# Seven-product stage: the upper weight part meets both parts of the rows in one 512-column matmul

## Chip, cores and metric

The kernel runs on one core of a Trainium2 chip. The metric is the device time of one execution in microseconds, here the median of three runs.

## What is computed

One layer of an encoder over 512 rows of 2048 channels, in float32: an RMS norm, one input projection into eight parts, a short gated convolution (branch A), a diagonal complex state-space recurrence (branch B), a gated merge, an output projection with a residual, and a final RMS norm. The change lies in branch A, which needs four of the projections (v, bg, cg, za), each 2048 x 2048:

```python
h = rmsnorm(x, norm_g)
proj = jnp.einsum('bld,dn->bln', h, w_in)
v, bg, cg, za, u, zb, ga, gb = jnp.split(proj, SPLITS, axis=-1)
ya = bg * causal_depthwise_conv(cg * v, conv_w)
ya = jnp.einsum('blc,cd->bld', ya * jax.nn.silu(za), w_out_a)
...
m = jax.nn.sigmoid(ga) * ya + jax.nn.sigmoid(gb) * yb
return x + jnp.einsum('bld,de->ble', m, w_o)
```

## The kernel before

Channels lie on the 128 partitions, the 512 rows (`L`) on the free axis. Every float32 product is made of three: a weight is split into an upper part `w_hi` (rounded, cast on ScalarE, line 544) and a lower part `w_lo` (the rest, subtracted on VectorE, line 561), and the rows into an upper and a lower part that lie side by side in one tile (`pair`, 128 x 2 x 512; `h_comb`, 128 x 2 x 2 x 256). Upper by upper, upper weight by lower rows, and lower weight by upper rows are summed in PSUM; the fourth is dropped. A weight tile `w_raw` of 128 x 1024 holds eight slices of 128 x 128; `WStream` loads it, casts and subtracts some products ahead, with four buffers each for `w_hi` and `w_lo`, so that the cast for the fourth product after this one waits until this one's last use of its `w_hi`.

The four projections of branch A take a stage of their own, after the gating products of branch B and the products of `wgb` (whose background work builds the combined rows) and before the products of `wga`. For a pair of column tiles (256 channels) a projection is a 2 x 2 block product: two halves of the 2048 inner channels, two halves of the 512 rows. Instead of eight block products it takes seven, with sums of weights (lines 491 to 500, on VectorE) and sums of rows (`T1` to `T4`, made in `combine` as `h_sum`, `h_t`, `h_comb`). `product` (line 911) multiplies one weight tile by 256 rows, eight slices of three matmuls of 256 columns. `seven` (line 921) calls it seven times: `pb`, `pd` and `pa` are halves of PSUM banks that several products share, running on without being cleared, and after each product ScalarE copies or VectorE adds its bank into a quarter of the result `o`. Eight pairs of column tiles times four projections make 32 calls of `seven`.

Behind each product one piece of background work is issued (`step`): the convolution (`conv`), the gate (`silu`), the gating and the write to DRAM (`out_a`). At the stage's end the eight results `yag` are read back from DRAM and split (`reload`, tiles `yag_r`), while four gate products run.

The engines work through their own instruction lists in order; a scheduler writes these lists and assigns buffers from pools. Of the pools, `tp` has five tiles of 128 x 512 (`tmp`), `r4b` four of 128 x 1024 (`wide`), opened when `uyp` closes after branch B; `psp` has the eight PSUM banks.

Of the kernel before, what the change touches and what calls it, by code (L numbers as in the profile page):

```python
# [16 lines left out]
P = 128  # L17
L = 512
# [559 lines left out]
def hybrid_kernel(ctx: ExitStack, tc: tile.TileContext, xT, x, cvec, fg, wu, wu7, wabc,  # L578
# [8 lines left out]
    tp = ctx.enter_context(tc.tile_pool(name="tp", bufs=5))  # L587
# [3 lines left out]
    uyp = tc.tile_pool(name="uyp", bufs=1)  # L591
    uyp_ctx = uyp.__enter__()

    def psum():
        t = psp.tile([P, L], F32, tag="ps", name="ps")
        return t

    c.psum = psum

    def tmp():  # L600
        t = tp.tile([P, L], F32, tag="tmp", name="tmp")
        return t
# [234 lines left out]
    for m in range(8):  # L837
        ps = psum()
        gemm(ps, yg)
        th, g = tmp(), tmp()  # L840
        act.activation(th, ps, AF.Tanh, scale=0.25, bias=bgh[:, m:m + 1])
        tt(g, yg[m][:, 0].bitcast(F32), yg[m][:, 1].bitcast(F32), ADD)
        stt(g, th, 1.0, g, ADD, MUL)
        tt(g, g, zb[m], MUL)
        b = pair()
        split(b, g)
        yb.append(b)
    uyp.__exit__(None, None, None)
    r4b = ctx.enter_context(tc.tile_pool(name="r4b", bufs=4))

    def wide(name, shape=(P, 2, L)):
        t = r4b.tile(list(shape), F32, tag="r4", name=name)
        return t
# [57 lines left out]
    def product(ps, acts, first, last):  # L911
        hi, lo = W.get()
        hi, lo = (w.rearrange("p (k n) -> p k n", n=P) for w in (hi, lo))
        for k in range(8):
            a = acts[k]
            nc.tensor.matmul(ps, hi[:, k], a[:, 0], start=first and k == 0, stop=False, skip_group_check=True)  # L916
            nc.tensor.matmul(ps, hi[:, k], a[:, 1], start=False, stop=False, skip_group_check=True)  # L917
            nc.tensor.matmul(ps, lo[:, k], a[:, 0], start=False, stop=last and k == 7, skip_group_check=True)  # L918
        step()

    def seven(name):

        o = wide(name)
        o11, o12, o21, o22 = o[:, 0, :HL], o[:, 0, HL:], o[:, 1, :HL], o[:, 1, HL:]
        pb, pd, pa = (psum()[:, :HL] for _ in range(3))
        product(pb, Y11, True, False)
        act.copy(o11, pb)
        product(pd, T1, True, False)
        act.copy(o22, pd)
        product(pb, T2, False, False)  # L930
        act.copy(o12, pb)
        product(pd, Y22, False, True)
        tt(o12, pd, o12, ADD)
        product(pb, T3, False, False)
        tt(o22, pb, o22, ADD)
        product(pa, Y21, True, True)
        tt(o11, pa, o11, ADD)
        product(pb, T4, False, True)
        act.copy(o21, pb)
# [247 lines left out]
```

## Time and profile before

| | |
|---|---|
| median of three runs | 1718.92 us (1717.94 to 1720.54) |
| the profiled execution | 1717.99 us |
| its span, first to last instruction | 1716.2 us |
| seven-product stage in it | 691.8 to 1337.2 us |
| busy, share of the span: TensorE, VectorE, ScalarE | 99%, 67%, 38% |

The profile shows one execution. A matmul row's duration reaches from its start to the end of its last column's way through the array, so neighbouring rows overlap, and the pace is read from start to start. VectorE's rows overlap a little in the same way. PEld is the loading of a weight slice into the array. "Idle before" names what ended the idle time of an engine. Names: `ps` is a PSUM bank, `w_sum` a tile with a sum of weights, `tmp`, `zb`, `cg`, `v`, `za`, `bg` SBUF tiles.

### The profile page before, as it was taken

The page shows a single profiled execution, that of the slowest core. Times are in us where ns is not written, and L with a number is a line of the kernel's source. Part 1 is how long each engine was busy: PE and PEld are TensorE (multiplying, and loading weights), DVE is VectorE, ACT ScalarE, POOL GpSimd, SP SyncE. Part 2 cuts the span into 40 slices and gives each one's busy share as a digit, 9 for nine tenths or more (in the row PEclk, how much of TensorE's full clock was granted, in tenths as well). Part 3 has the DMA queues.
Part 4 walks back from the last instruction along what each step waited for, and adds up shares of the span by engine and source line. Part 5 has one row for each costly group of instructions (what it writes and reads, how often), then busy time and mean ns, then how long its engine had stood idle before and what let it go on. Part 6 is the DMA issues. An engine that isn't in the chain of part 4 may idle for free.

```text
span 1716.2 us, 25344 instructions
## 1 busy us (share of the span) xinstructions
PE 1703.9 (99%) x10308; PEld 1530.4 (89%) x10308; DVE 1142.6 (67%) x1717; ACT 657.5 (38%) x883; POOL 130.5 (8%) x224
## 2 busy tenths in 40 slices
PE   9999999999999999999999999999999999999998
PEld 7888888888888888999999999999999888888887
DVE  7894584849759855687877777777878533333333
ACT  6434433233335422344444444444444422223321
POOL 0004212130100111000000000000000100010000
PEclk9999999999999999999999999999999999999999
DMA  8324334444441553333333333333344943363212
GB/s 299 123 86 130 126 121 114 146 123 142 124 122 50 184 160 129 105 99 119 114 119 121 108 111 99 111 111 123 102 129 132 340 158 111 111 234 124 78 43 98
DMA packets 65269, 222.18 MB, mean 129 GB/s; under 512 B 8896, under 2 KB 9024, under 8 KB 65152
## 3 DMA queue, kind: packets, MB, share of 16 engines
q1 hardware_dynamic: 49392, 170.94, 30.5%
q0 software_dynamic: 15040, 48.53, 9.1%
q8 instruction: 80, 1.31, 0.3%
q10 hardware_dynamic: 720, 1.10, 0.2%
q14 instruction: 37, 0.30, 0.1%
HBM read 195.24 MB, written 21.10 MB: 126 GB/s over the span
## 4 chain that ended last, share of the span: by engine, by line
PE 98%; DMA 1%; DVE 1%; ACT 0%; issue 0%; DVEq 0%; SPq 0%; ACTq 0%
PE ps L690 15%; PE ps L691 15%; PE ps L692 15%; PE ps L916 12%; PE ps L917 12%; PE ps L918 12%; PE ps L1040 3%; PE ps L1042 3%; PE ps L1041 3%; PE ps L767 1%; PE ps L768 1%; PE ps L769 1%; PE ps L338 1%; PE ps L433 1%; PE ps L347 1%; DMA yag_r<-yag 0%
## 5 line engine op out<-in xcount | busy, mean ns | idle before, releaser
L561 DVE TENSOR_TENSOR w_lo<-w_raw,w_hi 128x1024 fp32r<-128x1024 f32 (+2 forms) x341 | 412.6, 1213 | 340.8 <-ACT w_hi L544 340.5
L544 ACT CAST w_hi<-w_raw 128x1024 fp32r<-128x1024 f32 (+2 forms) x341 | 355.1, 1042 | 732.7 <-PE ps L691 368.4
L690 PE MATMUL ps<-pair,w_hi 128*128 128x512 f32 x1104 | 430.4, 390 | 0.0
L692 PE MATMUL ps<-pair,w_lo 128*128 128x512 f32 x1104 | 429.1, 389 | 0.6 <-DVE w_lo L561 0.6
L691 PE MATMUL ps<-pair,w_hi 128*128 128x512 f32 x1104 | 429.4, 389 | 0.0
L916 PE MATMUL ps<-h_comb,w_hi 128*128 128x256 f32 x1024 | 289.9, 283 | 0.1
L918 PE MATMUL ps<-h_comb,w_lo 128*128 128x256 f32 x1024 | 289.8, 283 | 0.0
L917 PE MATMUL ps<-h_comb,w_hi 128*128 128x256 f32 x1024 | 289.8, 283 | 0.0
L692 PEld LDWEIGHTS ps<-pair,w_lo 128*128 128x128 f32 x1104 | 207.2, 188 | 44.2 <-DVE w_lo L561 1.1
L690 PEld LDWEIGHTS ps<-pair,w_hi 128*128 128x128 f32 x1104 | 207.3, 188 | 42.7
L691 PEld LDWEIGHTS ps<-pair,w_hi 128*128 128x128 f32 x1104 | 207.3, 188 | 42.2
L917 PE MATMUL ps<-pair,w_hi 128*128 128x256 f32 x768 | 217.3, 283 | 0.0
L918 PE MATMUL ps<-pair,w_lo 128*128 128x256 f32 x768 | 217.3, 283 | 0.0
L916 PE MATMUL ps<-pair,w_hi 128*128 128x256 f32 x768 | 217.3, 283 | 0.0
L916 PEld LDWEIGHTS ps<-h_comb,w_hi 128*128 128x128 f32 x1024 | 196.6, 192 | 0.3 <-DVE bg L47 0.3
L917 PEld LDWEIGHTS ps<-h_comb,w_hi 128*128 128x128 f32 x1024 | 196.6, 192 | 0.0
L918 PEld LDWEIGHTS ps<-h_comb,w_lo 128*128 128x128 f32 x1024 | 196.6, 192 | 0.0
L916 PEld LDWEIGHTS ps<-pair,w_hi 128*128 128x128 f32 x768 | 147.5, 192 | 0.0
L917 PEld LDWEIGHTS ps<-pair,w_hi 128*128 128x128 f32 x768 | 147.5, 192 | 0.0
L918 PEld LDWEIGHTS ps<-pair,w_lo 128*128 128x128 f32 x768 | 147.5, 192 | 0.0
L544 ACT CAST w_hi<-w_sum 128x1024 fp32r<-128x1024 f32 x64 | 67.2, 1049 | 123.7 <-PE ps L917 114.9
L561 DVE TENSOR_TENSOR w_lo<-w_sum,w_hi 128x1024 fp32r<-128x1024 f32 x64 | 78.2, 1223 | 44.1 <-ACT w_hi L544 44.1
(204 smaller groups left out, 1909.2 us busy)
## 6 DMA issues: line engine op xcount, KB each, us to landing
w_raw<-in_wabc_dram SPq DMA_DIRECT2D x128, 512.0 KB, 3.6
w_raw<-in_wga_dram SPq DMA_DIRECT2D x64, 512.0 KB, 3.9
w_raw<-in_wgb_dram SPq DMA_DIRECT2D x48, 512.0 KB, 4.1
w_raw<-in_wo_dram SPq DMA_DIRECT2D x32, 512.0 KB, 3.6
w_raw<-in_wgz_dram SPq DMA_DIRECT2D x24, 512.0 KB, 3.7
w_raw<-in_wu_dram SPq DMA_DIRECT2D x15, 448.0 KB, 7.9
xt<-in_xT_dram SPq DMA_DIRECT2D x16, 256.0 KB, 6.8
ga<-tmp POOLq DMA_DIRECT2D x16, 256.0 KB, 2.3
```

The source lines that it names most:

```text
L338: nc.tensor.matmul(ps[:, i * NCH:(i + 1) * NCH], self.sl[ri][:, q].rearrange("p g s -> p (g s)"), self.u4[:, q, :], start=True, stop=True)
L544: nc.scalar.copy(hi[:, a:b], raw[:, a:b])
L561: nc.vector.tensor_tensor(out=lo[:, a:b], in0=raw[:, a:b], in1=hi.bitcast(F32)[:, a:b], op=SUB)
L690: nc.tensor.matmul(ps, hi[:, k], a[:, 0], start=first and k == 0, stop=False)
L691: nc.tensor.matmul(ps, hi[:, k], a[:, 1], start=False, stop=False)
L692: nc.tensor.matmul(ps, lo[:, k], a[:, 0], start=False, stop=last and k == 7)
L916: nc.tensor.matmul(ps, hi[:, k], a[:, 0], start=first and k == 0, stop=False, skip_group_check=True)
L917: nc.tensor.matmul(ps, hi[:, k], a[:, 1], start=False, stop=False, skip_group_check=True)
L918: nc.tensor.matmul(ps, lo[:, k], a[:, 0], start=False, stop=last and k == 7, skip_group_check=True)
L1040: nc.tensor.matmul(ps, a[:, 0, cs], hi[:, k2, c0:c1], start=first and k2 == 0, stop=False)
L1041: nc.tensor.matmul(ps, a[:, 0, cs], lo[:, k2, c0:c1], start=False, stop=False)
L1042: nc.tensor.matmul(ps, a[:, 1, cs], hi[:, k2, c0:c1], start=False, stop=last and k2 == 1)
```

## The change

`product` now multiplies a slice of the upper weight by both parts of the rows in one matmul of 512 columns: the upper rows go to the first half of a bank, the lower rows to the second. The lower weight's matmul adds 256 columns onto the second half. A product therefore fills a whole bank, and its value is the sum of the two halves. `seven` copies and adds whole banks into two scratch tiles (`half`: `e1`, `e2`) and adds the halves only at the end, with one operation for each column tile, into `o`. For the scratch tiles the pool `r4b` has six tiles instead of four; the pool `tp` is closed before it opens, and `tmp` then takes tiles of `r4b`.

```diff
-    tp = ctx.enter_context(tc.tile_pool(name="tp", bufs=5))
...
+    uyp, tp = tc.tile_pool(name="uyp", bufs=1), tc.tile_pool(name="tp", bufs=5)
+    uyp_ctx, tp_ctx = uyp.__enter__(), tp.__enter__()
+    r4b = None
...
     def tmp():
-        t = tp.tile([P, L], F32, tag="tmp", name="tmp")
+        if r4b:
+            return wide("tmp")[:, 0]
+        t = tp_ctx.tile([P, L], F32, tag="tmp", name="tmp")
         return t
...
+    tp.__exit__(None, None, None)
     uyp.__exit__(None, None, None)
-    r4b = ctx.enter_context(tc.tile_pool(name="r4b", bufs=4))
...
+    r4b = ctx.enter_context(tc.tile_pool(name="r4b", bufs=6))
...
     def product(ps, acts, first, last):
         hi, lo = W.get()
         hi, lo = (w.rearrange("p (k n) -> p k n", n=P) for w in (hi, lo))
+        both = ps.rearrange("p (h l) -> p h l", h=2)
         for k in range(8):
             a = acts[k]
-            nc.tensor.matmul(ps, hi[:, k], a[:, 0], start=first and k == 0, stop=False, skip_group_check=True)
-            nc.tensor.matmul(ps, hi[:, k], a[:, 1], start=False, stop=False, skip_group_check=True)
-            nc.tensor.matmul(ps, lo[:, k], a[:, 0], start=False, stop=last and k == 7, skip_group_check=True)
+            nc.tensor.matmul(both, hi[:, k], a, start=first and k == 0, stop=False,
+                             skip_group_check=True)
+            nc.tensor.matmul(both[:, 1], lo[:, k], a[:, 0], start=False, stop=last and k == 7,
+                             skip_group_check=True)
         step()
...
-        o11, o12, o21, o22 = o[:, 0, :HL], o[:, 0, HL:], o[:, 1, :HL], o[:, 1, HL:]
-        pb, pd, pa = (psum()[:, :HL] for _ in range(3))
+        e1, pb = wide("half"), psum()
         product(pb, Y11, True, False)
-        act.copy(o11, pb)
+        act.copy(e1[:, 0], pb)
+        e2, pd = wide("half"), psum()
         product(pd, T1, True, False)
-        act.copy(o22, pd)
+        act.copy(e2[:, 1], pd)
         product(pb, T2, False, False)
-        act.copy(o12, pb)
+        act.copy(e1[:, 1], pb)
         product(pd, Y22, False, True)
-        tt(o12, pd, o12, ADD)
+        tt(e1[:, 1], pd, e1[:, 1], ADD)
         product(pb, T3, False, False)
-        tt(o22, pb, o22, ADD)
+        tt(e2[:, 1], pb, e2[:, 1], ADD)
+        pa = psum()
         product(pa, Y21, True, True)
-        tt(o11, pa, o11, ADD)
-        product(pb, T4, False, True)
-        act.copy(o21, pb)
+        tt(e1[:, 0], pa, e1[:, 0], ADD)
+        for i, e in enumerate((e1, e2)):
+            if i:
+                product(pb, T4, False, True)
+                act.copy(e2[:, 0], pb)
+            v = e.rearrange("p b (h l) -> p b h l", h=2)
+            tt(o[:, i].rearrange("p (b l) -> p b l", b=2), v[:, :, 0], v[:, :, 1], ADD)
         return o
```

TensorE's list where one product ends and the next begins, before (the rows of a product are `pair` or `h_comb`):

```order
L916 MATMUL ps<-pair,w_hi 128x256
L917 MATMUL ps<-pair,w_hi 128x256
L918 MATMUL ps<-pair,w_lo 128x256
L916 MATMUL ps<-h_comb,w_hi 128x256
L917 MATMUL ps<-h_comb,w_hi 128x256
L918 MATMUL ps<-h_comb,w_lo 128x256
```

and now:

```order
L924 MATMUL ps<-pair,w_lo 128x256
L922 MATMUL ps<-pair,w_hi 128x512
L924 MATMUL ps<-pair,w_lo 128x256
L922 MATMUL ps<-h_comb,w_hi 128x512
L924 MATMUL ps<-h_comb,w_lo 128x256
```

Three matmuls for each slice have become two, a long and a short one in turn.

VectorE's list in one call of `seven`, from the sum of weights behind the third product, before:

```order
L491 TENSOR_TENSOR w_sum<-w_raw 128x1024
L47 TENSOR_TENSOR cg<-ps,cg 128x256
L495 TENSOR_TENSOR w_raw<-w_raw 128x1024
L561 TENSOR_TENSOR w_lo<-w_raw,w_hi 128x1024
L47 TENSOR_TENSOR cg<-ps,cg 128x256
L496 TENSOR_TENSOR w_raw<-w_sum,w_raw 128x1024
L561 TENSOR_TENSOR w_lo<-w_sum,w_hi 128x1024
L47 TENSOR_TENSOR cg<-ps,cg 128x256
L500 TENSOR_TENSOR w_sum<-w_raw 128x1024
L561 TENSOR_TENSOR w_lo<-w_raw,w_hi 128x1024
L561 TENSOR_TENSOR w_lo<-w_sum,w_hi 128x1024
```

and now:

```order
L47 TENSOR_TENSOR half<-ps,half 128x512
L561 TENSOR_TENSOR w_lo<-w_raw,w_hi 128x1024
L495 TENSOR_TENSOR w_raw<-w_raw 128x1024
L47 TENSOR_TENSOR half<-ps,half 128x512
L496 TENSOR_TENSOR w_raw<-w_sum,w_raw 128x1024
L561 TENSOR_TENSOR w_lo<-w_sum,w_hi 128x1024
L47 TENSOR_TENSOR half<-ps,half 128x512
L500 TENSOR_TENSOR w_sum<-w_raw 128x1024
L47 TENSOR_TENSOR cg<-half 128x512
L561 TENSOR_TENSOR w_lo<-w_raw,w_hi 128x1024
L47 TENSOR_TENSOR cg<-half 128x512
L561 TENSOR_TENSOR w_lo<-w_sum,w_hi 128x1024
```

The three additions out of PSUM are twice as wide, and two additions of halves (`cg<-half`) stand before and behind a subtraction for lower weights.

VectorE's list at the end of the stage, in the last `seven` (result `bg`), before:

```order
L47 TENSOR_TENSOR pair<-yag_r,pair 128x512 x2
L47 TENSOR_TENSOR bg<-ps,bg 128x256
L47 TENSOR_TENSOR pair<-yag_r,pair 128x512
L561 TENSOR_TENSOR w_lo<-w_raw,w_hi 128x1024
L47 TENSOR_TENSOR pair<-yag_r,pair 128x512
```

and now:

```order
L47 TENSOR_TENSOR bg<-half 128x512
L561 TENSOR_TENSOR w_lo<-w_raw,w_hi 128x1024 x2
L47 TENSOR_TENSOR bg<-half 128x512
L47 TENSOR_TENSOR pair<-yag_r,pair 128x512
L47 TENSOR_TENSOR bg<-bg,cg 128x1024
L47 TENSOR_TENSOR pair<-yag_r,pair 128x512 x7
```

The splits of the rows read back (`yag_r`), which stood between the last result's additions, now stand behind them.

## Rows read from the trace of the kernel before

**Rows 1.** The page: busy us (share of the span) and instructions of each engine.

```profile
PE 1703.9 (99%) x10308; PEld 1530.4 (89%) x10308; DVE 1142.6 (67%) x1717; ACT 657.5 (38%) x883; POOL 130.5 (8%) x224
```

**Rows 2.** Busy us of engines in two stretches: the stage, about one pair.

```profile
core 0: us, PE busy (x) PEld busy (x) DVE busy (x) ACT busy (x) POOL busy (x), PEclk, DMA share, GB/s
691.50:1337.20 645.70, 645.64 (x5379) 645.36 (x5379) 501.58 (x510) 290.15 (x381) 6.42 (x12) 1.00 0.37 116
934.00:1015.00 81.00, 81.00 (x677) 81.00 (x676) 63.25 (x64) 36.36 (x48) 0.53 (x1) 1.00 0.36 111
```

**Rows 3.** Waits in the stage: engine, line <- releaser: us, times, longest.

```profile
DVE w_lo L561 <- ACT w_hi L544: 141.7, 113, 4.2
...
PEld ps L916 <- DVE bg L47: 0.3, 1, 0.3
```

**Rows 4.** Timeline of TensorE, last 512s and first 256s: start us, us, instruction.

```profile
690.41 0.39 PE L690 MATMUL ps<-pair,w_hi 128*128 128x512 f32 x1
...
691.77 0.28 PE L916 MATMUL ps<-pair,w_hi 128*128 128x256 f32 x1
691.88 0.28 PE L917 MATMUL ps<-pair,w_hi 128*128 128x256 f32 x1
692.00 0.28 PE L918 MATMUL ps<-pair,w_lo 128*128 128x256 f32 x1
692.12 0.28 PE L916 MATMUL ps<-pair,w_hi 128*128 128x256 f32 x1
...
694.64 0.28 PE L916 MATMUL ps<-h_comb,w_hi 128*128 128x256 f32 x1
```

**Rows 5.** Two lines' matmuls: duration ns min/median/max, first and last start, forms.

```profile
L916 PE MATMUL ps<-pair,w_hi x768: 277/283/283, 691.8 to 1333.6; 128*128 128x256 f32 x192
...
L1040 PE MATMUL ps<-w_hi_r,pair x60: 277/389/389, 1663.6 to 1706.0; 128*128 128x512 f32 x36, 128*128 128x256 f32 x24
```

**Rows 6.** Timeline of TensorE, last 256s of the stage and first 512s behind it.

```profile
1337.08 0.28 PE L918 MATMUL ps<-h_comb,w_lo 128*128 128x256 f32 x1
1337.20 0.40 PE L690 MATMUL ps<-pair,w_hi 128*128 128x512 f32 x1
1337.43 0.40 PE L691 MATMUL ps<-pair,w_hi 128*128 128x512 f32 x1
...
1338.58 0.39 PE L690 MATMUL ps<-pair,w_hi 128*128 128x512 f32 x1
```

**Rows 7.** Timeline of VectorE: 512-wide, 256-wide and 1024-wide operations, and the convolution's.

```profile
539.52 0.68 DVE L55 SCALAR_TENSOR_TENSOR zb<-tmp,ps 128x512 f32<-128x512 f32 x1
540.12 0.68 DVE L47 TENSOR_TENSOR pair<-tmp,pair 128x512 fp32r<-128x512 f32 x1
...
945.89 0.42 DVE L47 TENSOR_TENSOR cg<-ps,cg 128x256 f32<-128x256 f32 x1
946.22 1.22 DVE L495 TENSOR_TENSOR w_raw<-w_raw 128x1024 f32<-128x1024 f32 x1
947.35 1.22 DVE L561 TENSOR_TENSOR w_lo<-w_raw,w_hi 128x1024 fp32r<-128x1024 f32 x1
...
979.24 2.07 DVE L55 SCALAR_TENSOR_TENSOR cg<-v,cvec_t,cg 128x511 f32<-128x511 f32 x3
```

**Rows 8.** Timeline of ScalarE: 512 and 256 columns out of PSUM, a cast.

```profile
692.70 0.59 ACT L817 ACTIVATE tmp<-ps 128x512 f32<-128x512 f32 x1
694.78 1.05 ACT L544 CAST w_hi<-w_raw 128x1024 fp32r<-128x1024 f32 x1 [1.49 <-PE ps L917]
695.73 0.37 ACT L927 COPY cg<-ps 128x256 f32<-128x256 f32 x1
```

**Rows 9.** DMA issues: count, KB each, median us from issue to landing.

```profile
tmp<-gb POOLq DMA_DIRECT2D x16, 256.0 KB, 3.7
...
yag<-bg POOLq DMA_DIRECT2D x8, 512.0 KB, 4.1
yag_r<-yag POOLq DMA_DIRECT2D x8, 512.0 KB, 4.9
```

**Rows 10.** Timeline of VectorE: the last combined rows before the stage.

```profile
673.35 1.29 DVE L47 TENSOR_TENSOR h_comb<-h_t,h_comb 128x512 fp32r<-128x512 f32 x2
```

More of the change, by code (lines that the diff above doesn't have):

```diff
@@ L590, in hybrid_kernel @@
     c.r4 = ctx.enter_context(tc.tile_pool(name="r4", bufs=NR4))
-    uyp = tc.tile_pool(name="uyp", bufs=1)
-    uyp_ctx = uyp.__enter__()
+    uyp, tp = tc.tile_pool(name="uyp", bufs=1), tc.tile_pool(name="tp", bufs=5)
+    uyp_ctx, tp_ctx = uyp.__enter__(), tp.__enter__()
+    r4b = None
     def psum():
@@ L598, in hybrid_kernel, with wide @@
     c.psum = psum
+    def wide(name, shape=(P, 2, L)):
+        t = r4b.tile(list(shape), F32, tag="r4", name=name)
+        return t
     def tmp():
-        t = tp.tile([P, L], F32, tag="tmp", name="tmp")
+        if r4b:
+            return wide("tmp")[:, 0]
+        t = tp_ctx.tile([P, L], F32, tag="tmp", name="tmp")
         return t
@@ L847, in hybrid_kernel @@
         yb.append(b)
+    tp.__exit__(None, None, None)
     uyp.__exit__(None, None, None)
-    r4b = ctx.enter_context(tc.tile_pool(name="r4b", bufs=4))
-    def wide(name, shape=(P, 2, L)):
-        t = r4b.tile(list(shape), F32, tag="r4", name=name)
-        return t
+    r4b = ctx.enter_context(tc.tile_pool(name="r4b", bufs=6))
     th7 = []
```

## The prediction

> **What bounds the kernel now.** I read the busy time of the engines first, then the table of stretches for the seven-product stage, the waits inside that stage, and last the starts of single matmuls. TensorE is busy for 99% of the span [rows 1], and in the stage for 645.64 of 645.70 us, at a granted clock of 1.00, the 2.4 GHz level [rows 2]. The only wait of TensorE in the whole stage is one of 0.3 us; the long wait there is VectorE's, 141.7 us in 113 pieces, for the casts of the upper weight part on ScalarE [rows 3]. So the stage lasts as long as TensorE's string of matmuls, and the change has to be priced as time from one matmul's start to the next. The durations of single rows (0.28 and 0.39 us) overlap and can't be added.
>
> From 692.12 to 694.64, 21 matmuls of 256 columns start: 2.52 / 21 = 120.0 ns each. From 690.41 to 691.77, 6 matmuls of 512 columns: 1.36 / 6 = 226.7 ns each [rows 4]. The stage has 1024 + 768 = 1792 groups of three (7 products x 8 slices x 32 results), so 5376 x 120.0 ns = 645.1 us, which is the stretch. Two matmuls of 256 cost 240.0 ns where one of 512 costs 226.7.
>
> **The change, TensorE.** A group is now one matmul of 512 and one of 256: the same 768 columns, but two instructions and two weight loads instead of three. The two kinds never alternate in the kernel before, so the price has to come from places where one kind follows the other. Right after a string of 512s, the first 256 has its successor 0.11 us behind it and not 0.12: at 691.77 and 691.88 [rows 4]. It is also the shorter one: the matmuls of the stage last 283 ns but the shortest 277, and a 277 comes once more, on the line that begins with 256s behind 512s in the last stage [rows 5]. 120 less those 6 is 114, and half of 226.7 is 113.3; that is how I read the 0.11: per column a lone 256 costs what a 512 costs, and 120.0 is what a long string of 256s costs because each new weight load has only one short matmul to hide behind. In the changed kernel every 256 follows a 512, so its own weights are loaded with time to spare. Then a group costs 226.7 + 113.3 = **340.0 ns** instead of 360.0, and 1792 x 20.0 ns = **35.8 us** go.
>
> The other end is the steady price of each kind, 226.7 + 120.0 = 346.7 ns; then 1792 x 13.3 ns = 23.8 us go. For this end speaks the passage the other way: after the string of 256s, the starts of the first six 512s are 1337.20 to 1338.58, 230 ns each, and the first of them is 0.23 us long in step [rows 6]. If a 512 behind a 256 always costs 3 to 7 ns more, the sum lies between the two ends or at this one. I take 340.0, because the two rows of a 256 behind a 512 show exactly the order that the change makes, and in the passage of rows 6 the first 512 stands behind a long string, not behind a single 256.
>
> The moving operand of the new matmul is two runs of 256 columns that do not touch (in a pair the lower part lies 512 elements behind the upper). No matmul before has such an operand. Bounds: nothing, or a second start for the second run, 2 x 120.0 = 240.0 ns in place of 226.7. I take nothing, since the runs are as long as whole matmuls now and the lower end is nearer to how one instruction streams; the upper end is a rival below. The half that the second matmul adds to was last written 256 columns earlier, as before, so no new distance between two additions to one element arises.
>
> One rule speaks against the change. The Trainium skill, page "TensorE: Matmul & The Clock Gate", section "Back-to-back issue gap", gives the gap of matmuls in a row as columns / 2.4 plus 2.5 ns; by that, a merge would save 2.5 ns a group, an estimate of 4.5 us and a time of 1714.4. The rows differ by 13.3 ns, and the measurement decides. The same section of the Trainium skill says that in a stream of load and matmul both set the spacing, which agrees with 0.11 against 0.12 us.
>
> **The change, VectorE.** Per result, three additions out of PSUM grow from 256 to 512 columns, and two additions of the halves come in. Durations overlap here too, so I take steps: a 256-wide addition out of PSUM 0.33 us (945.89 to 946.22), a 1024-wide operation 1.13 [rows 7], a 512-wide one reading PSUM 0.60 (539.52 to 540.12) [rows 7]. A pair of column tiles (four results) gains 12 x 0.27 + 8 x 0.60 = 8.0 us. The halves are read as two runs of 256; at worst that is two 256-wide steps, 0.66. In the pair of rows 2 VectorE is busy 63.25 of 81.00 us; it becomes 71.3, against 28 products x 8 x 340.0 ns = 76.2 us of TensorE. That still hides, with 5 us to spare, but the cover is thin, so I walk one result's queue. Time 0 is the end of the third product, a product is 2.72 us. Lower weights until 2.1 (the cast takes 0.95 first [rows 8]), weight sum until 3.2, addition of the fourth product until 3.8, lower weights and a weight difference until 6.1, addition of the fifth until 6.7, two of 1.13 until 9.0, addition of the sixth until 9.6, weight difference, first halves, lower weights until 12.5, second halves (behind the copy of the seventh product) until 13.1. The one that TensorE waits for soonest is the addition of the fifth product: the seventh product writes on in the same bank from 8.16. The margin is 8.16 - 6.7 = 1.5 us; behind the convolution's five operations, 1.13 + 4 x 0.69 = 3.9 us [rows 7], I get 1.1. The lower weights are ready about two products early. So VectorE costs TensorE nothing in the middle; for small slips at the ends of the stage I put 1 us.
>
> **The change, ScalarE and buffers.** Four copies a result grow from 256 to 512 columns, from 0.37 to 0.59 us by the nearest row (a Tanh out of PSUM) [rows 8]: 128 x 0.22 = 28 us on an engine that is busy 290.15 of 645.70 us [rows 2]. Hidden; the soonest reader, the product after next on that bank, comes 2.72 us later. The pool of wide tiles opens only when the pool of the small ones closes. So the sums of the rows (h_sum, h_t) now start after the gating products, and the first loads of gb go out together behind the last use of a small tile; a load takes 3.7 us [rows 9]. Both are covered: lower weights for three products of 5.4 us are ready, PSUM has eight banks, and the combined rows were complete at 674.6 [rows 10], 20 us before the first product on them at 694.64 [rows 4]. At the stage's end the reloads of yag now stand behind the last result on VectorE and ScalarE instead of between its additions. Copy, halves, gating (3 us), writing and reading back (4.1 + 4.9 us [rows 9]) and two splits come to some 15 us; four gate products, 24 matmuls of 226.7 ns each, give 21.8 us, and the first half of the next product 5.4 more. The 0.3 us of rows 3 goes.
>
> **Sum.** The profiled execution took 1717.99 us (span 1716.2 and 1.8 around it); 1717.99 - 35.8 + 1 = 1683.2. The median lies 0.93 above the profiled one: **1684 us**.
>
> **Rivals.**
> 1. Steady prices (346.7 ns): 1718.9 - 23.8 + 1 = 1696. For it: 120.0 holds over thousands of matmuls, 0.11 stands in two places only; and rows 6. Chance 0.33.
> 2. The second run costs a second start, the change doesn't do what it says: a group stays between 353 and 360 ns, and 1792 x 7 ns = 12.5 us or nothing goes: 1706 to 1719. Against it: one instruction and one load go in any case. (The 1714.4 by the Trainium skill's "TensorE: Matmul & The Clock Gate" would lie in this case.) Chance 0.10, of it 0.04 within 0.2% of before.
> 3. VectorE takes over, and it ends slower. Its 141.7 us of waits are 17.7 a pair. An in-order queue that stops for casts at the wrong places keeps some of them; 71.3 plus what it keeps is then the pair's time. From 9.4 us kept (80.7 is TensorE's pair now) the kernel is no faster; with two thirds kept, 83.1 us a pair, the seventh product waits for its bank in every result, 8 x 2.4 = 19 us are lost, and the time is 1738. Against it: a cast can begin as soon as the product four before its own has ended, so a late VectorE finds it done. Chance 0.06 for slower; a milder form (2 to 9 us a pair kept, 1686 to 1716) 0.07.
> 4. More than forecast, under 1680: it would need columns faster than any string of 512 shows. Chance 0.03.
>
> **How the numbers follow.** The forecast has 0.41, with 1681 to 1688 of its own; rivals 0.33, 0.10, 0.13 and 0.03. The range 1680 to 1707 holds the forecast, rival 1, most of the mild form of rival 3 (0.05) and the edge of rival 2, and leaves out 0.20: the rest of these, rival 4 and slower. A measurement of this kernel can tell some 0.2% (3.4 us) from no change: faster 0.89 (0.41 + 0.33 + 0.06 + 0.06 + 0.03), same 0.05, slower 0.06.
>
> **What would show it.** In the profile after: starts of the new pairs 340 ns apart in sum (226.7 then 113.3; with 120.0 rival 1; with about 240 rival 2), the stage 609 us long, TensorE's busy share there still 99% or more, VectorE near 570 us in it, its waits for casts down to some 40 us. A wait of TensorE on VectorE in each result would be rival 3. The forecast is wrong if the steps are 340 but the stage isn't 609 us: then a wait ate it.

## The result, and the profile of the changed kernel

The changed kernel takes **1707.37 us** (median of 4 runs, 1706.39 to 1708.14) against 1719.45 (4 runs beside it, 1717.94 to 1720.54): ratio 0.993, 95% interval 0.9913 to 0.9947. It is faster by 12.1 us. The forecast was 1684, a gain of 35 us, with a range that ended at 1707. The sign and the place are right; two thirds of the gain are missing.

The page of the changed kernel, first line of busy times, answers to [rows 1]:

```profile
PE 1693.8 (99%) x8516; PEld 1437.5 (84%) x8516; DVE 1202.0 (70%) x1781; ACT 684.9 (40%) x883; POOL 130.4 (8%) x224
```

1792 matmuls and as many weight loads are gone (10308 to 8516), and TensorE is still busy for 99% of the span. The table of stretches, for the stage and for the same 81 us inside it as in [rows 2]:

```profile
core 0: us, PE busy (x) PEld busy (x) DVE busy (x) ACT busy (x) POOL busy (x), PEclk, DMA share, GB/s
693.70:1326.90 633.20, 633.20 (x3586) 549.77 (x3585) 558.14 (x570) 314.89 (x376) 5.88 (x11) 1.00 0.36 117
934.00:1015.00 81.00, 81.00 (x461) 70.29 (x460) 72.34 (x75) 40.87 (x49) 0.53 (x1) 1.00 0.36 117
```

The stage lasts from 693.73 to 1326.89, where the first matmul behind it starts: 633.16 us, where it lasted 645.43 (691.77 to 1337.20). The 12.3 us of difference are as much as the whole gain of the medians. TensorE is busy in all of it, at the same granted clock of 1.00: no wait took the rest. The spans of the two profiled executions lie only 9.9 us apart (1716.2 and 1706.3), since the stage begins 2.0 us later in the changed one. The cause lies in the first 20 us, where its granted clock was 0.91, and in the kernel before 1.00 (same columns; the kernel before, then the changed one):

```profile
0.00:20.00 20.00, 16.61 (x70) 13.39 (x71) 11.30 (x18) 14.16 (x22) 0.88 (x5) 1.00 0.92 337
0.00:20.00 20.00, 16.86 (x61) 13.61 (x62) 10.72 (x17) 12.21 (x19) 0.88 (x5) 0.91 0.92 335
```

In both, TensorE had waited some 2 us there for ScalarE; in the changed one a part of what followed ran at the 1.2 GHz level. It is not the change's doing: `e1_contig` below has the change too, and its profile shows 1.00 in these 20 us.

The waits of the stage (engine, line <- releaser: us, times, longest) have no row of TensorE any more, and VectorE's waits for casts have halved from the 141.7 of [rows 3]:

```profile
DVE w_lo L561 <- ACT w_hi L544: 68.1, 52, 4.2
...
DVE half L47 <- PE ps L924: 1.9, 3, 0.7
```

So each group of matmuls costs more than forecast: 633.16 us / 1792 = **353.3 ns**, not 340.0. The timeline of TensorE at the stage's start (start us, us, instruction) shows it from the second group on:

```profile
693.73 0.39 PE L922 MATMUL ps<-pair,w_hi 128*128 128x512 f32 x1
693.95 0.28 PE L924 MATMUL ps<-pair,w_lo 128*128 128x256 f32 x1
694.07 0.40 PE L922 MATMUL ps<-pair,w_hi 128*128 128x512 f32 x1
694.30 0.28 PE L924 MATMUL ps<-pair,w_lo 128*128 128x256 f32 x1
694.42 0.40 PE L922 MATMUL ps<-pair,w_hi 128*128 128x512 f32 x1
694.66 0.28 PE L924 MATMUL ps<-pair,w_lo 128*128 128x256 f32 x1
694.78 0.40 PE L922 MATMUL ps<-pair,w_hi 128*128 128x512 f32 x1
695.01 0.28 PE L924 MATMUL ps<-pair,w_lo 128*128 128x256 f32 x1
695.13 0.40 PE L922 MATMUL ps<-pair,w_hi 128*128 128x512 f32 x1
```

Read the starts of L922. From 693.73 to 694.07 the first group takes 0.34 us, as forecast. The next take 0.35, 0.36, 0.35. With the exact starts of the trace the stage repeats a pattern of three groups to its end: 233 + 117, 241 + 120, 236 + 113 ns, together 1060. The first 512 stands behind a 512; every later one stands behind a 256, and its duration is 0.40 instead of 0.39. The averages over the stage are 236.5 ns from a 512 to the 256 behind it and 116.9 from a 256 to the next 512.

### The profile page after: what moved, and what is told of

The parts are those of the page before. It is cut to its first block, busy times and chain, and to the rows that moved or that the text cites. A ratio compares the mean times of both kernels' runs of the same rounds, so it can differ in the third digit from the quotient of the medians.

```text
span 1706.3 us, 21911 instructions
## 1 busy us (share of the span) xinstructions
PE 1693.8 (99%) x8516; PEld 1437.5 (84%) x8516; DVE 1202.0 (70%) x1781; ACT 684.9 (40%) x883; POOL 130.4 (8%) x224
## 4 chain that ended last, share of the span: by engine, by line
PE 98%; DMA 1%; DVE 0%; ACT 0%; SPq 0%; issue 0%; DVEq 0%
PE ps L922 25%; PE ps L698 15%; PE ps L696 15%; PE ps L697 15%; PE ps L924 12%; PE ps L1054 3%; PE ps L1052 3%; PE ps L1053 3%; PE ps L773 1%; PE ps L774 1%; PE ps L775 1%; PE ps L433 1%; PE ps L338 1%; PE ps L347 1%; PE ps L430 0%; DMA w_raw<-in_wu_dram 0%
## 5 line engine op out<-in xcount | busy, mean ns | idle before, releaser
L696 PE MATMUL ps<-pair,w_hi 128*128 128x512 f32 x1104 | 431.1, 391 | 0.0
L697 PE MATMUL ps<-pair,w_hi 128*128 128x512 f32 x1104 | 430.1, 390 | 0.0
L922 PE MATMUL ps<-h_comb,w_hi 128*128 128x512 f32 x1024 | 366.2, 399 | 0.0
L922 PE MATMUL ps<-pair,w_hi 128*128 128x512 f32 x768 | 275.7, 399 | 0.0
L696 PEld LDWEIGHTS ps<-pair,w_hi 128*128 128x128 f32 x1104 | 207.5, 188 | 42.4
L697 PEld LDWEIGHTS ps<-pair,w_hi 128*128 128x128 f32 x1104 | 207.4, 188 | 42.4
L922 PEld LDWEIGHTS ps<-h_comb,w_hi 128*128 128x128 f32 x1024 | 192.8, 188 | 47.6
L922 PEld LDWEIGHTS ps<-pair,w_hi 128*128 128x128 f32 x768 | 144.6, 188 | 35.7
L1052 PE MATMUL ps<-w_hi,pair 128*128 128x512 f32 (+1 forms) x212 | 81.8, 386 | 0.0
L1053 PE MATMUL ps<-w_lo,pair 128*128 128x512 f32 (+1 forms) x212 | 81.7, 386 | 0.0
L1054 PE MATMUL ps<-w_hi,pair 128*128 128x512 f32 (+1 forms) x212 | 81.7, 386 | 0.0
L47 DVE TENSOR_TENSOR half<-ps,half 128x512 f32<-128x512 f32 x96 | 65.6, 683 | 1.9 <-PE ps L924 1.9
```

The lines of the kernel that those rows point to most:

```text
L47: return v.tensor_tensor(out=o, in0=a, in1=b, op=op)
L922: nc.tensor.matmul(both, hi[:, k], a, start=first and k == 0, stop=False, skip_group_check=True)
L1052: nc.tensor.matmul(ps, a[:, 0, cs], hi[:, k2, c0:c1], start=first and k2 == 0, stop=False)
L1053: nc.tensor.matmul(ps, a[:, 0, cs], lo[:, k2, c0:c1], start=False, stop=False)
L1054: nc.tensor.matmul(ps, a[:, 1, cs], hi[:, k2, c0:c1], start=False, stop=last and k2 == 1)
```

## Experiments

The question: why 353.3 ns and not 340.0 (the forecast) or 346.7 (rival 1)? The group times below are worked out from starts, over the stage or over a stretch without stops.

**Is it the operand in two runs, or the bank?** Rival 2 had named 353 ns, for a second start of the second run. `e1_contig` lays the two parts of the combined rows side by side, so that their operand is one run of 512; `pair` stays in two runs.

```
-            act.copy(p[:, 0], t[:, 2 * i:2 * i + 2])
-            tt(p[:, 1], t[:, 2 * i:2 * i + 2], p[:, 0].bitcast(F32), SUB)
-            o += [p[:, :, 0], p[:, :, 1]]
+            act.copy(p[:, :, 0], t[:, 2 * i:2 * i + 2])
+            tt(p[:, :, 1], t[:, 2 * i:2 * i + 2], p[:, :, 0].bitcast(F32), SUB)
+            o += [p[:, 0], p[:, 1]]
```

> The changed kernel, but the combined rows (h_comb) are stored so that upper and lower part lie behind one another; the operand of 1024 of the 1792 groups is then one run of 512, that of the other 768 (pair) stays two runs. In the changed kernel a group takes 353.3 ns (starts of the 512 and the 256 behind it: 236.5 + 116.9) on both. Theory A (the second run of the operand costs a second start): groups on h_comb fall to about 340 ns, groups on pair stay at 353; the stage gets 1024 x 13.3 = 13.6 us shorter, the time about 1694. Theory B (a 512 that follows a 256 is slower, whatever its runs): both stay at 353.3, the time stays at 1707.

Measured: 1706.59 us, ratio 0.9929 (0.9914 to 0.9944), stage 633.16 us. Groups on one run and groups on two runs both take 236.4 + 116.9 ns. The layout costs nothing; of the two theories, B held.

`e3_hionly` keeps that layout and leaves the lower weight's matmuls out of the stage, so that only 512s remain.

```
             a = acts[k]
-            nc.tensor.matmul(both, hi[:, k], a, start=first and k == 0, stop=False, ...
-            nc.tensor.matmul(both[:, 1], lo[:, k], a[:, 0], start=False, stop=last and k == 7, ...
+            nc.tensor.matmul(both, hi[:, k], acts[k], start=first and k == 0, stop=last and k == 7, ...
```

> The changed kernel without the products of the lower weight in this stage (their matmuls are left out, the weights are still prepared), and with h_comb stored in one run of 512: only 512-column matmuls are left, on pair with two runs and on h_comb with one. Theory A: 240 ns from start to start on pair, 226.7 on h_comb. Theory B: 226.7 on both. The product is then 1.8 us long while VectorE has some 2.3 us of work for each (71.3 us a pair of column tiles / 28 and more), so TensorE should wait for VectorE and the stage should be 570 us or a little more.

Measured: 1642.56 us, one run, the stage 569 us. Between the stops of TensorE, a 512 in two runs and one in one run both take 227.0 ns (median), which is the 226.7 of [rows 4]; theory B held. TensorE now waits, for casts on ScalarE above all, and from 690 to 1270 us the granted clock was 0.93 on average. The rows say whose turn it would be if TensorE got this much faster:

```profile
PEld ps L921 <- ACT w_hi L544: 91.0, 76, 3.1
...
PE ps L921 <- ACT w_hi L544: 62.5, 54, 2.7
```

`e12_half0` adds the lower weight's product to the first half of the bank instead of the second (the sum of the halves is the same), so that no 256 adds to what the 512 just ahead wrote last. No instruction moves on any engine.

```
-            nc.tensor.matmul(both[:, 1], lo[:, k], a[:, 0], ...
+            nc.tensor.matmul(both[:, 0], lo[:, k], a[:, 0], ...
```

> The changed kernel with the product of the lower weights added to the first half of the bank instead of the second (the sum of the halves is the same); no instruction moves on any engine. Theory A (the extra 13.3 ns of a group are the price of two kinds of matmul with a weight load each): 353.3 ns a group, 1707 us. Theory B (the extra comes from adding to the half that the matmul just ahead wrote last): the 256 finds its half written 512 columns ago, so its step falls to 113.3 and the group to 340 to 347 ns, 1684 to 1696 us, or the 512 behind it gets longer instead by the same amount.

Measured: 1707.42 us, ratio 0.9928 (0.9911 to 0.9944), 353.3 ns a group, the same three-group pattern. Theory A held, theory B falls.

**Is it the alternation?** The edits of three kernels change only the order of the 16 matmuls of a product: eight 512s and then eight 256s (`e2_group`), two and two (`e4_aabb`), four and four (`e11_a4b4`). The scheduler moved a few operations of VectorE and ScalarE as well, but TensorE's stops in the three stages come to under 0.4 us each. For two and two:

```
-        for k in range(8):
-            a = acts[k]
-            nc.tensor.matmul(both, hi[:, k], a, ...)
-            nc.tensor.matmul(both[:, 1], lo[:, k], a[:, 0], ...)
+        for k in range(0, 8, 2):
+            for i in (k, k + 1):
+                nc.tensor.matmul(both, hi[:, i], acts[i], ...)
+            for i in (k, k + 1):
+                nc.tensor.matmul(both[:, 1], lo[:, i], acts[i][:, 0], ...)
```

> The changed kernel with another order in a product: all eight 512-column matmuls on the upper weight first, then all eight 256-column ones on the lower. Theory B: 512s in a row take 226.7, 256s in a row 120, and only one passage a product is left: (8 x 226.7 + 8 x 120.0) = 2773 ns plus some 27 ns for the passage back, 350 ns a group, stage 627 us, time about 1701; without a price of the passage 621 us and 1695. Theory A: 8 x 240 + 8 x 120 = 2880 ns a product, stage 645 us, time about 1719.

> The changed kernel with two slices taken together: two 512s, then the two 256s. Half as many passages as in the changed kernel. Theory B, with the passage as the thing that costs (353.3 - 340.0 = 13.3 ns or, against the steady 346.7, 6.7 ns a passage pair): between 343 and 350 ns a group, stage 616 to 627 us, time 1690 to 1701. Theory A: no difference to the changed kernel, 353, time 1707.

> Four matmuls of 512 with upper weights, then four of 256 with lower ones, twice in each product. Theory A (every change from 256 back to 512 costs some 3 to 7 ns, and a settled string costs 226.7 and 120.0): between the 348.3 ns a group of two and two and the 349.1 of eight and eight, 1697 to 1701 us. Theory B (the first two or three 256s behind 512s have the short step of 113.3, so the best length is where these make the largest share): at most 346 ns a group, 1694 or less.

| order in a product | ns a group | us | ratio to before |
|---|---|---|---|
| one and one (the change) | 353.3 | 1707.37 | 0.993 (0.9913 to 0.9947) |
| two and two | 348.3 | 1697.76 | 0.9877 (0.9863 to 0.9892) |
| four and four | 351.0 | 1703.71 | 0.9906 (0.9891 to 0.992) |
| eight and eight | 349.1 | 1700.83 | 0.9891 (0.9875 to 0.9908) |

Order alone is worth 9.6 us. Theory B of `e2_group` and of `e4_aabb` held in time and stage. But four and four is slower than both its neighbours, which a price per change of kind can't give: both theories of `e11_a4b4` missed. The timeline of eight and eight:

```profile
800.01 2.00 PE L921 MATMUL ps<-pair,w_hi 128*128 128x512 f32 x8
801.85 1.11 PE L924 MATMUL ps<-pair,w_lo 128*128 128x256 f32 x8
802.80 0.40 PE L921 MATMUL ps<-h_comb,w_hi 128*128 128x512 f32 x1
```

Eight 512s take 1.84 us, 230 ns each. By the exact starts the five behind the 256s take 233, 236, 228, 233 and 231, and only then it is 227. The eight 256s begin with 113 and 119 and then take 120. So the 113 that the forecast took for the price of a 256 behind a 512 is the first step of a passage, and the passage back costs about 27 ns, spread over five 512s. That passage stood in [rows 6]. Such steps need no 256s, either: in `e3_hionly`, where the stage has only 512s, behind a stop of TensorE near the stage's start, and the long step right after it, the next steps are 231, 236, 228, 233 and 230 before it is 227 again.

**Is it the length of the second matmul?** Four kernels change its columns: 128 and 192 (`e5_n128`, `e6_n192`; part of the lower weight's product is left out), 320 and 384 (`e7_n320`, `e8_n384`; it multiplies columns of both row parts, so another sum). For 128:

```
-            nc.tensor.matmul(both[:, 1], lo[:, k], a[:, 0], start=False,
+            nc.tensor.matmul(both[:, 1, :128], lo[:, k], a[:, 0, :128], start=False,
```

> The changed kernel with the lower weight's matmul cut to the first 128 of its 256 columns (the other half of that product is left out); order and count of instructions as in the changed kernel, where a group takes 353.3 ns. Theory L (while a weight is loaded the next matmul waits, and a short matmul cannot hide the load behind it): what stands behind the 512 stays as long as the load, some 126.7 ns, a group stays near 353. Theory P (columns plus a price for each instruction or passage): 128 columns are 53 to 57 ns less, a group is 297 to 300.

> The same with 192 of 256 columns. Theory L: near 353. Theory P: 353.3 less 64 columns, 325 to 327 ns.

> The changed kernel with the lower weight's matmul made longer, 320 columns in two runs of 160 (of both parts of the rows; the sum formed is another one than the product). Theory L: 320 columns at the rate of a 512 (226.7 / 512 a column) are 141.7 ns, longer than the load; nothing is left over and a group is 368. Theory P: 353.3 plus 64 columns, 380 to 382.

> The same with 384 columns in two runs of 192. Theory L: 226.7 + 170 = 397. Theory P: 353.3 plus 128 columns, 407 to 410.

| second matmul | 128 | 192 | 256 | 320 | 384 |
|---|---|---|---|---|---|
| ns a group | 340.0 | 340.0 or 344.3 | 353.3 | 376.7 | 406.7 |
| columns of both / 2.4 GHz | 266.7 | 293.3 | 320.0 | 346.7 | 373.3 |

From 256 on, a group costs its columns and 30 to 33 ns; 226.7 for a 512 and 120.0 for a 256 are each 13.3 above their columns, so 3 to 7 ns of the 30 to 33 are left for the alternation. With 128 and 192 columns no stretch between stops averages under 340.0. The timeline of the kernel with 128:

```profile
801.27 0.44 PE L922 MATMUL ps<-pair,w_hi 128*128 128x512 f32 x1
801.55 0.22 PE L924 MATMUL ps<-pair,w_lo 128*128 128x128 f32 x1
801.61 0.44 PE L922 MATMUL ps<-pair,w_hi 128*128 128x512 f32 x1
```

Here 0.28 us pass from a 512 to the 128 and 0.06 from there to the next 512. With 192, some stretches between two stops take a steady 340.0 and others a steady 344.3 (the second in a pattern of three groups, 1033 ns), with the same instructions: an uneven price that comes up again below. Theory P is near above (376.7 against 380 to 382, 406.7 against 407 to 410) and wrong below; theory L has the floor right, though not its height, and is wrong above. So 340.0 does exist, but as a floor that 256 columns are too long to reach. The kernels with 128 and 192 took 1720.38 and 1726.82 us all the same, because TensorE waited. The waits of the first:

```profile
PEld ps L922 <- DVE half L47: 29.7, 31, 2.0
PE ps L922 <- DVE half L47: 21.6, 31, 1.8
```

The scheduler had also set VectorE's operations in another order there, so this is no clean test of VectorE at 340 ns.

**Is VectorE's cover thin?** `e10_dve2` does each addition of halves twice.

```
             tt(o[:, i].rearrange("p (b l) -> p b l", b=2), v[:, :, 0], v[:, :, 1], ADD)
+            tt(o[:, i].rearrange("p (b l) -> p b l", b=2), v[:, :, 0], v[:, :, 1], ADD)
```

> The changed kernel with each addition of halves done twice (same result): 64 x 0.60 = 38 us more of VectorE in the stage. My theory (VectorE's work is hidden in the changed kernel, with 79.1 us of TensorE a pair against some 69.8 of VectorE, then 74.6): the stage stays at 633 us, the time within 1705 to 1709. Rival (VectorE's margin is already used up, and a part of the missing gain is its): the stage grows by 8 us or more, with waits of TensorE on the line of the additions, 1715 or more.

Measured: 1719.91 us, ratio 1.0003 (0.9994 to 1.0013). My theory missed, and the rival's 8 us or more came about: with some 38 us of added VectorE work (64 steps of 0.60) the stage grew from 633.16 to 647.44 us. TensorE stood idle for 14.8 us, the difference in this row of the stretch table (us, TensorE busy):

```profile
692.20:1339.70 647.50, 632.74 (x3586) 1.00 0.34 114
```

Counted from start to start, the stops cost 19.8 us; why the stage grew by only 14.3 is told below. More of it stood behind ScalarE's copies than behind additions (line <- releaser):

```profile
PEld ps L922 <- ACT half L933: 12.0, 8, 1.9
...
PE ps L922 <- ACT half L933: 9.4, 7, 1.6
PEld ps L922 <- DVE half L47: 8.8, 11, 1.4
ACT tz L966 <- DVE za L47: 6.4, 8, 0.9
...
PE ps L922 <- DVE half L47: 5.3, 8, 1.1
```

In all eight stops for a copy of line 933, one in each pair, the copy stood in ScalarE's queue behind the gate's activation (`tz`), and this had waited for VectorE's last addition of the halves of `za`, one of those that the run does twice. ScalarE's timeline at one of them:

```profile
999.29 1.06 ACT L966 ACTIVATE tz<-za 128x1024 f32<-128x1024 f32 x1 [0.89 <-DVE za L47]
1000.25 0.57 ACT L933 COPY half<-ps 128x512 f32<-128x512 f32 x1
```

Here too some casts and VectorE operations were set in another order. In the changed kernel VectorE costs TensorE nothing, but the 4.8 us a pair that this run added did not fit, in the order that it had.

The same run showed what I had not looked for. Behind two stops of the same length, released by the copy of the same line, the same matmuls run on in two ways:

```profile
1000.87 0.50 PE L922 MATMUL ps<-h_comb,w_hi 128*128 128x512 f32 x1 [1.57 <-ACT half L933]
...
1001.32 0.40 PE L922 MATMUL ps<-h_comb,w_hi 128*128 128x512 f32 x1
1001.55 0.28 PE L924 MATMUL ps<-h_comb,w_lo 128*128 128x256 f32 x1
1001.67 0.39 PE L922 MATMUL ps<-h_comb,w_hi 128*128 128x512 f32 x1
...
1002.71 0.40 PE L922 MATMUL ps<-h_comb,w_hi 128*128 128x512 f32 x1
```

```profile
1082.41 0.50 PE L922 MATMUL ps<-h_comb,w_hi 128*128 128x512 f32 x1 [1.57 <-ACT half L933]
...
1082.87 0.40 PE L922 MATMUL ps<-h_comb,w_hi 128*128 128x512 f32 x1
1083.10 0.28 PE L924 MATMUL ps<-h_comb,w_lo 128*128 128x256 f32 x1
1083.22 0.40 PE L922 MATMUL ps<-h_comb,w_hi 128*128 128x512 f32 x1
...
1084.28 0.40 PE L922 MATMUL ps<-h_comb,w_hi 128*128 128x512 f32 x1
```

Four groups take 1.39 us in the first (347 ns each) and 1.41 in the second (353), and each goes on so until the next stop, 86 groups later: means of 346.7 and 353.4. About half of the stretches of this run are of each kind: some 810 groups at 346.7 give back 5.4 of the 19.8 us, which is why the stage grew by 14.3.

**Two rhythms?** `f1_entries` puts one or two extra matmuls (overwritten later) ahead of the first product of each result, 16 entries of different lengths, each twice; `f2_entries_aabb` does so in the order two and two.

```
+    EXTRA = [[n] * r for r in (1, 2) for n in (64, 128, 192, 256, 320, 384, 448, 512)] * 2
...
+        for n in EXTRA.pop(0) if first and acts is Y11 else ():
+            a = acts[0]
+            d, s = (both[:, 0, :n], a[:, 0, :n]) if n <= HL else (both[:, :, :n // 2], a[:, :, :n // 2])
+            nc.tensor.matmul(d, hi[:, 0], s, start=True, stop=True, skip_group_check=True)
```

> The changed kernel with one or two extra matmuls of 64 to 512 columns (their sums are overwritten) ahead of the first product of each of the 32 results, 16 different entries, each twice. Theory R (two rhythms of the same string, chosen at its start): stretches of seven products at a steady 346.7 ns a group and others at 353.3, the same entry from the same rhythm leading to the same one both times. Theory P (353.3 is the price of alternation, and the faster stretches came from VectorE's lateness): 353.3 behind every entry, and about 1711 us (some 4 us for the extra matmuls).

> The kernel with two 512s, then two 256s, and the same entries ahead of each result. Theory R: besides 348.3 ns a group another steady value in some stretches, 346.7 or lower. Theory P: 348.3 behind every entry, about 1702 us.

Measured in `f1_entries`, ns a group behind each entry, over products two to seven, the same both times that an entry came:

| extra columns | 64 | 128 | 192 | 256 | 320 | 384 | 448 | 512 |
|---|---|---|---|---|---|---|---|---|
| one extra | 353.3 | 346.7 | 346.7 | 346.7 | 353.3 | 346.7 | 353.3 | 346.7 |
| two extra | 346.7 | 353.3 | 353.3 | 353.3 | 353.3 | 346.7 | 346.7 | 346.7 |

Nothing lies between. Theory R holds: the string has two rhythms, and what goes ahead of it decides which it keeps. (Each entry came behind the same one both times, except the first.) At 346.7 a group costs its columns and 26.7 ns, twice the 13.3 from above: the fast rhythm leaves nothing for the alternation. With 32 extra pieces of work the kernel took 1706.61 us, no more than the changed kernel. In the order two and two every entry led to 348.3 (1706.45 us with the extra work), as theory P of `f2_entries_aabb` had it: no other rhythm showed.

Can it be entered once, on purpose? `g1_start256`, `g2_start384` and `g3_start512x` keep only an entry at the stage's start, `EXTRA = [[256]] + [[]] * 31` and the like (two of 512 in the third). `h1_rhythm` repeats the first two entries of `f1_entries`, `[[64], [128]] + [[]] * 30`.

> The changed kernel with one extra matmul of 256 columns at the stage's start (its sum is overwritten), nothing else. Theory R (the start chooses the rhythm, which then holds): if it enters the fast one, 346.7 ns a group through the whole stage, 621 us, and 1707.4 - 1792 x 6.7 ns = 1695.5 us; if it enters the slow one, 1707.5. Rival (something else in the stage brings the string back to the slow rhythm): a fast stretch at first, then 353.3; between 1700 and 1707.

> The same with 384 columns, an entry that led to the fast rhythm four times of four inside the stage (once and doubled). Theory R: 1695 to 1696 us. Rival: 1700 to 1707, with a change of rhythm in the stage.

> The same with two of 512 columns. At the stage's start they only lengthen the string of 512s ahead of it, so they don't change how the alternation is entered. Theory R: the slow rhythm as in the changed kernel, 353.3 ns and some 1707.8 us. If the mere presence of extra work there were what helps: 1696.

> The changed kernel with an extra matmul of 64 columns ahead of the first result and one of 128 ahead of the second (their sums are overwritten), none after that: the first two entries of the run with 32. Theory R (a rhythm, once entered, holds until the string is disturbed): the first result at 353.3 ns a group, the other 31 at 346.7; 31 x 56 groups x 6.7 ns = 11.6 us less than the changed kernel, stage 621.6 us, time about 1696. Rival (the fast rhythm needs new entries to last): back to 353.3 after some results, 1700 to 1707.

The first three took 1707.69, 1707.83 and 1707.21 us, 353.3 ns through the whole stage: behind a string of 512s these entries lead into the slow rhythm. Theory R of `g2_start384` (1695 to 1696 us) missed. As a test of whether the start chooses they say little; they show that an entry's effect depends on what ran ahead of it: all three led to the fast rhythm inside the stage. `h1_rhythm` took **1696.95 us**, ratio 0.9874 (0.9857 to 0.989), as theory R had it. No operation of VectorE or ScalarE moved. Its timeline at the second result, and 600 us later at the stage's end:

```profile
711.06 0.40 PE L928 MATMUL ps<-h_comb,w_hi 128*128 128x512 f32 x1
711.30 0.28 PE L930 MATMUL ps<-h_comb,w_lo 128*128 128x256 f32 x1
711.41 0.40 PE L928 MATMUL ps<-h_comb,w_hi 128*128 128x512 f32 x1
711.64 0.28 PE L930 MATMUL ps<-h_comb,w_lo 128*128 128x256 f32 x1
711.76 0.22 PE L925 MATMUL ps<-pair,w_hi 128*128 128x128 f32 x1
711.82 0.45 PE L928 MATMUL ps<-pair,w_hi 128*128 128x512 f32 x1
712.10 0.28 PE L930 MATMUL ps<-pair,w_lo 128*128 128x256 f32 x1
712.22 0.39 PE L928 MATMUL ps<-pair,w_hi 128*128 128x512 f32 x1
712.45 0.28 PE L930 MATMUL ps<-pair,w_lo 128*128 128x256 f32 x1
712.57 0.39 PE L928 MATMUL ps<-pair,w_hi 128*128 128x512 f32 x1
...
1313.34 0.39 PE L928 MATMUL ps<-h_comb,w_hi 128*128 128x512 f32 x1
1313.57 0.28 PE L930 MATMUL ps<-h_comb,w_lo 128*128 128x256 f32 x1
1313.69 0.39 PE L696 MATMUL ps<-pair,w_hi 128*128 128x512 f32 x1
```

Ahead of the one matmul of 128 columns a 512 lasts 0.40 us in the record, behind it 0.39, and from 712.22 to 1313.69 the starts lie 230 + 117 ns apart, through 31 results. Two small matmuls that compute nothing save 10.4 us against the changed kernel. By their times `e4_aabb` (1697.76) and `h1_rhythm` (1696.95) can't be told apart, though in the traces the stage of `h1_rhythm` is 2.4 us shorter (621.8 and 624.2 us); both beat both kernels, and `e4_aabb` needs no luck with an entry.

**Do the buffers matter?** `e9_pools` is the kernel before with the change's pools only: the pool of small tiles closed with its neighbour, six wide tiles, small tiles taken out of them.

```
...
+    tp.__exit__(None, None, None)
...
-    r4b = ctx.enter_context(tc.tile_pool(name="r4b", bufs=4))
...
+    r4b = ctx.enter_context(tc.tile_pool(name="r4b", bufs=6))
```

> The kernel before with only the change of the pools (the pool of small tiles closed with its neighbour, six wide tiles, small tiles taken out of them); the three matmuls of 256 stay. My theory (the buffers cost and bring nothing): 1718 to 1720 us, the stage 645 us as before. Rival (the pools give back or take a part of the change's gain, in the stretch ahead of the stage or behind it): 3 us or more away from that, in either direction, with the difference outside the stage.

Measured: 1718.3 us, ratio 0.9996 (0.9986 to 1.0005), the stage 645.1 us. The pools bring and cost nothing that can be told: the interval reaches from 2.4 us faster to 0.9 slower.

## Why the prediction was wrong, and where it was right

**The term that failed** is the price of a group. The prediction wrote 226.7 + 113.3 = 340.0 ns, 1792 x 20.0 = 35.8 us; measured are 353.3 ns, 1792 x 6.7 = 12.0 us. The rest of the sum stands: take 12.0 in place of 35.8 and 1717.99 - 12.0 + 1 + 0.93 gives 1707.9, against 1707.37. The 1 us put for slips of VectorE did not show, as TensorE has no wait in the stage.

Two choices led there. The 113.3 came from one matmul behind a long string of 512s [rows 4]. The successor there starts 0.11 us later, but the next one 0.12 again; such a step belongs to the passage, as `e2_group` shows (113, 119, 120). The changed kernel has 226 and 113 together in its first group alone; later a 113 comes only behind a 512 of 236. And the passage the other way [rows 6] was set aside because the first 512 stood behind a long string. Its six steps of 230 were the better witness: in the changed kernel every 512 but the first stands behind a 256. The reason given for the 113.3, that a lone 256 hides its weight load better, is not borne out: with 320 and 384 columns in the second matmul, the surplus over the columns stays at 30 to 33 ns.

**Rival 1** (346.7 ns, 1696 us) was the better reading of a steady string. The group does run at 346.7, in the fast of two rhythms, and with two entries to bring it there the time is 1696.95. Its steps are then 230 and 117, though, not the 226.7 and 120.0 that rival 1 added up; why the sums agree is not shown. The changed kernel enters the slow rhythm, behind the 512s of the stage ahead, and stays in it, with no stop of TensorE in the stage. No view of the kernel before, in which the two kinds never alternate, could show which.

**Rival 2** named 353 to 360 ns and 1706 to 1719, and the time fell there, but for another reason. The second run is free (`e1_contig`, `e3_hionly`), as the prediction took it.

**The page's rule.** The Trainium skill, page "TensorE: Matmul & The Clock Gate", section "Back-to-back issue gap", puts a gap of 2.5 ns on each matmul beside its columns; the prediction's estimate by it was 1714.4. The section gives this for single matmuls and says that in a stream of load and matmul, which this stage is, both set the spacing. The saving of a merge is 6.7 ns a group in one rhythm and 13.3 in the other, so the rule's 2.5 ns is too small for both, and the 20.0 of the forecast by rows too large. The second sentence says nothing on the size. That it agrees with 0.11 against 0.12 us, as the prediction has it, is not shown: the 0.11 is a step of the passage.

**VectorE, ScalarE, buffers** came out as walked through. VectorE's busy time in the stage is 558 us, forecast near 570; waits for casts are 68 us, forecast some 40 for a stage 24 us shorter; TensorE never waits for it. ScalarE's grew by 24.7 us (290.15 to 314.89), forecast 28, all hidden. The 0.3 us of [rows 3] went. **Rival 3** did not come about, but its mechanism is near: with 38 us more of VectorE's work, stops of TensorE cost 19.8 us (`e10_dve2`), more than half of it by copies on ScalarE that stood behind the gate's activation, which waited for VectorE, a path that the walk through one result's queue left out. In the prediction's own numbers the milder form would begin later than it says: with 2 us a pair kept, 71.3 + 2 is still under 76.2. Whether the margin of 1.1 to 1.5 us would have held at 340 ns stays open, as groups of 256 never ran at that.

**What stays open** is why there are two rhythms. The slow one stays with another layout of the operand (`e1_contig`) and another half written (`e12_half0`), and in `f1_entries` both run with no wait that the trace shows. With 192 columns there are two as well; with 320 and 384 one showed, in a string that was never stopped.

## What to carry to other kernels

A price read at the one place where two kinds of instruction meet is the price of that passage; for a string that alternates, look at the passages in both directions, and widen the range for a rhythm that no view can show. Where TensorE is the bound and matmuls of two lengths alternate, try orders (two and two was worth 9.6 us here) before anything larger. Where the steps of a string are not what either kind costs alone, list them exactly over some groups: a steady pattern with a surplus may be one of two rhythms.

## What the runs showed of the hardware

- A string of one 512 and one 256 runs at 346.7 or at 353.3 ns a group (230 + 117, or 1060 ns for three groups), with the same instructions in the same order. Extra matmuls ahead of it decide, the same entry behind the same one with the same outcome; a rhythm once entered held for 31 results, 600 us (`f1_entries`, `h1_rhythm`). With 192 columns in place of the 256 the two values are 340.0 and 344.3 (`e6_n192`).
- Two and two kept one rhythm of 348.3 ns a group behind all 32 entries (`f2_entries_aabb`).
- With eight of each in turn, behind 256s five 512s take 228 to 236 ns before the step is 226.7 again, and behind 512s two 256s take 113 and 119 before it is 120.0 (`e2_group`). Behind a stop, 512s take such steps too (`e3_hionly`).
- A 512 and a shorter matmul, each with its own weights, took no less than 340.0 ns together, with 128 columns as with 192 (`e5_n128`, `e6_n192`).
- A moving operand of 512 columns in two runs that don't touch takes what one run takes: 227.0 ns (`e3_hionly`).
